# Nine raw chunks in the ring instead of six, four split halves instead of six, and shared slots for two small tiles

## The chip, the cores and the metric

The kernel runs on one core of a Trainium2 chip. The core has TensorE (PE in the profile) with its weight loads (PEld), VectorE (DVE), ScalarE (ACT), GpSimd (POOL) and SyncE (SP), which here mostly issues DMAs. The metric is the device time of one execution in microseconds (us), median of several runs. All weights and activations are fp32.

## The reference

A model of two parts works on one sequence of 512 tokens, 1024 wide. The first part has two layers with a linear recurrence, latent attention and a dense feed-forward; the second has a matrix LSTM mixer and then a mixture of 32 experts, of which each token takes four. The change touches the expert part alone:

```
logits = xt @ w_router + b_router
top_vals, top_idx = top_k(logits, 4);  top_gates = softmax(top_vals)
# per expert e, for the tokens xb routed to it:
gate = min(xb @ w_gate[e] + b_gate[e], 7)
up   = clip(xb @ w_up[e] + b_up[e], -7, 7)
y    = (gate * sigmoid(1.702 * gate) * (up + 1)) @ w_down[e] + b_down[e]
out[token] += top_gate * y
```

Each expert has 12 MB of weights (gate, up and down, each 1024 x 1024 in fp32), so 32 of them are read once each.

## The kernel before

**Experts and blocks.** A router stage counts the tokens of each expert and ranks the experts by count. Each rank has a fixed number of slots: two blocks of 128 slots for the two fullest, then 128 and 64 slots for three, one block of 128 for seven (the last rank, 31, runs first), and one block of 64 for the other twenty. The lists for this case are `FEW` (L1920); a second list stands behind a branch on a flag `many` (L1798, L1801) for inputs with another spread, and is not run here. The order of the ranks is fixed by hand: mostly two 64-slot experts, a 128-slot expert, two 64-slot experts, and then one with two blocks, and so on.

**Chunks and halves.** The weights of an expert are 12 chunks of 1 MB, each a tile of 128 x 2048: four for the first half of gate and up, four for the second, four for down. `split_ahead` (L1583) loads a chunk into the next slot of a ring of `NRAW` tiles named `raw` (DMA on SP's queue, L1591; slots `RAW0` of which lie in a pool opened early) and treats it as two halves.

- For an expert with 128 or more slots each half is *split*: ACT rounds it to a tile `w` in the fast fp32 form of PE (L244) and DVE writes the remainder beside it (L245). These pairs live in a ring of `AHEAD + 1` slots, `EARLY` of which lie in the pool opened early. The products are then whi, wlo and the remainder of x (`product`, `lin`: matmuls at L236, named gu<-w,xth, gu<-w,xtl and dn<-w,hTh, dn<-w,hTl).
- A 64-slot expert (`twin`) multiplies the raw half directly in plain fp32 (gu<-raw,xf and dn<-raw,hf, 128 x 64 columns against 128 x 512), so that it needs no split.

`weights` (L1601) is called once for each half that PE takes. It first tops up the halves in hand to `AHEAD + 1`, counting raw ones too, then emits one or more of the small steps waiting in `later` (`catch_up`), and hands out the oldest half.

**Stages.** `ranked` (L1815) goes through the experts in this order: first half of gate and up of the current expert, down of the one before, second half of gate and up of the current one. Between the matmuls of a stage it places the small steps: `find` (L1513: which tokens, and the gather of their rows from DRAM by POOL, L1529, into xg), `fetch` (L1534: transposes of xg at L1538 into tps, then xf for a 64-slot block, xn for the 64-slot half block of a 128 + 64 expert, xth and xtl for 128 slots) and `turn` (L1690: transposes of the activated product u at L1698 into hf, hn or hTh and hTl). The results `g` (L1668 for a 64-slot expert, L1687 otherwise) and u belong to the activation; yy (L1741, L1760) is the scaled output that POOL scatters into DRAM.

**What sets the order.** PE's instructions stand in the order of the Python code. ACT, DVE, POOL and SP are ordered by a scheduler which simulates the program, and then run in that order, each instruction waiting for its own inputs. A DMA into a ring slot waits on SP until the last reader of that slot is done: PE's last matmul for a raw chunk, DVE's second split for a split chunk. DMAs behind it on SP wait with it.

Of the kernel before, what the change touches and what calls it, by code (L numbers as in the profile page):

```python
# [6 lines left out]
F32 = mybir.dt.float32  # L7
F32R = mybir.dt.float32r
# [9 lines left out]
P = 128  # L18
T = 512
D = 1024  # L20
KD = D // P
# [184 lines left out]
class _Kernel:  # L206
# [1327 lines left out]
    def fetch(self, b):  # L1534


        nc, mo, n = self.nc, self.mo, b["n"]
        turned = lambda tp, k, i: nc.tensor.transpose(tp[:, i * n:(i + 1) * n], b["x"][0:n, k * P:(k + 1) * P],  # L1538
                                                      self.ident[0:n, 0:n])

        def small():
            tp = self.tps()
            for k in range(KD):
                turned(tp, k, k)
            if b["twin"]:
                b["xt"] = xt = mo.tile([P, KD, n], F32, tag="xf", name="xf", bufs=2)
                nc.scalar.activation(xt.rearrange("p k s -> p (k s)"), tp, AF.Copy)  # L1547
            else:
                b["xt"] = xt = mo.tile([P, KD, P], F32R, tag="xn", name="xn", bufs=2)
                self.split(tp.rearrange("p (k s) -> p k s", k=KD), xt[:, :, 0:n], xt[:, :, n:P])  # L1550

        def part(c):
            if c == 0:
                self.nx += 1
                b["xt"] = [x[:, self.nx % 2] for x in self.xts]
            tp = self.tps()
            for k in range(4):
                turned(tp, 4 * c + k, k)
            self.split(tp, *(x[:, 512 * c:512 * c + 512] for x in b["xt"]))

        return [small] if n == 64 else [lambda: part(0), lambda: part(1)]

    def rings(self, z):


        nraw, nw = (NRAW - RAW0, AHEAD + 1 - EARLY) if z else (RAW0, EARLY)
        self.raws += list(self.wp[z].tile([P, nraw, 2048], F32, name="raw").rearrange("p n c -> n p c"))
# [15 lines left out]
    def split_ahead(self, n):  # L1583

        nc = self.nc
        while self.todo and len(self.halves) < n:
            src, i, whole = self.todo.pop(0)
            if i == 0:
                self.raw = self.raws[self.nload % NRAW]
                self.nload += 1  # L1590
                nc.sync.dma_start(self.raw, src)  # L1591
            raw = self.raw[:, 1024 * i:1024 * i + 1024]
            if whole:
                self.halves.append((raw, None))
                continue
            w = self.ws[self.nsplit % (AHEAD + 1)]
            self.nsplit += 1
# [3 lines left out]
    def weights(self):  # L1601
        self.split_ahead(AHEAD + 1)
        self.catch_up(CU + len(self.later) // CV)
        return self.halves.pop(0)
# [85 lines left out]
    def turn(self, blocks, n):  # L1690

        nc, mo = self.nc, self.mo
        self.catch_up()
        for b in blocks:
            m, u = b["n"], b["u%d" % n]
            tp = self.tps()
            for k in range(4):
                nc.tensor.transpose(tp[:, k * m:(k + 1) * m], u[:, k * P:(k + 1) * P], self.ident[0:m, 0:m])  # L1698
            if b["twin"]:
                h = mo.tile([P, 4, m], F32, tag="hf", name="hf", bufs=3)  # L1700
                nc.scalar.activation(h.rearrange("p k s -> p (k s)"), tp[:, 0:256], AF.Copy)
            elif m == 64:
                h = mo.tile([P, 4, P], F32R, tag="hn", name="hn", bufs=2)
                self.split(tp[:, 0:256].rearrange("p (k s) -> p k s", k=4), h[:, :, 0:m], h[:, :, m:P])
            else:
                h = self.pair(mo, [P, T], "hT", bufs=4)
                self.split(tp, *h)
            b["h%d" % n] = h
# [61 lines left out]
    def first_weights(self):  # L1770
# [4 lines left out]
        self.queue(self.chosen[0][0] + self.chosen[0][1])  # L1775
        self.split_ahead(EARLY)

    def experts(self):
# [7 lines left out]
        self.find(b, lambda j: self.gate0[:, j])  # L1786
        self.split_ahead(AHEAD + 1)
        self.down_bias_rows()
# [86 lines left out]
            self.catch_up()  # L1875

    def finish_start(self):
        self.nf = self.mo.tile([P, D], F32, tag="xn", name="nf", bufs=2)
        self.nc.scalar.dma_start(self.nf, self.a["nfrow"].to_broadcast([P, D]))  # L1879

    def finish(self):
# [20 lines left out]

SILU7 = 11.914 / (1.0 + _np.exp(-11.914))
ASIDE = (3, 1)
NRAW = 6
RAW0 = 4
XG = 2
EARLY = 3
CU = 1
CV = 6  # L1910
SGB = 2

AHEAD = 5

SLOTS = [(128, 128)] * 2 + [(128, 64)] * 5 + [(128,)] * 9 + [(64,)] * 15 + [(128,)]

# [55 lines left out]
```

## Time and profile before

| | |
|---|---|
| median of 3 runs | 2970.43 us (2966.03 to 2973.55) |
| profiled execution | 2969.97 us, span on the core 2968.2 us |
| expert part | 1685 to 2941 us of the span |
| PE busy | 2761.0 us, 93% of the span |
| DVE, ACT busy | 1581.2 us (53%), 1119.6 us (38%) |
| raw<-in_wgu, raw<-in_wd | 256 and 128 transfers of 1024 KB; 9.4 and 9.7 us from issue to landing (median) |

Busy PE means that a matmul is in flight, at whichever clock was granted; PE at 93% therefore includes slow matmuls. The expert part is not uniform: the shares of DMA and PE change with the kind of expert, which the table by stretches below shows. In the rows, a number in front is the start in us, the next one how long it lasted, and brackets behind a row give the idle time before it and what released it.

### The profile page before, as it was taken

How to read it: one execution, taken by the hardware profiler on the slowest of the kernel's cores; microseconds unless marked ns; L12 is line 12 of the kernel's file. 1: busy time of each engine (PE TensorE's matmuls, PEld its weight loads, DVE VectorE, ACT ScalarE, POOL GpSimd, SP SyncE). 2: the span in 40 equal slices, each digit the busy share in tenths (PEclk: the TensorE clock that was granted, in tenths of full speed). 3: DMA queues.
4: the chain of work that ended last, by engine and by line, in shares of the span. 5: the costliest groups of instructions: out<-in, count | busy, mean ns of one | idle time of the engine just before them, and what ended most of it. 6: DMA issues, size and time to landing. Idle time of an engine off the chain costs nothing. (4 is left out here: it accounts for less than half of the span.)

```text
span 2968.2 us, 33708 instructions
## 1 busy us (share of the span) xinstructions
PE 2761.0 (93%) x12644; PEld 1936.7 (65%) x12644; DVE 1581.2 (53%) x2601; ACT 1119.6 (38%) x1655; POOL 206.8 (7%) x206
## 2 busy tenths in 40 slices
PE   7999999999999999999999699899899899889885
PEld 5677888888777788888777456454546445446452
DVE  7977575465776653334688543353533434434343
ACT  4644432223564442223353433342423334334342
POOL 0101000000100000000011010111001011010000
PEclk9999999999999999999999799999999999999998
DMA  5332456464221323332214486988987997997997
GB/s 226 122 119 93 156 180 205 142 211 135 86 68 56 95 89 92 100 100 89 89 50 178 172 301 243 405 316 328 382 329 289 398 384 270 404 384 269 394 347 261
DMA packets 126367, 634.93 MB, mean 214 GB/s; under 512 B 14448, under 2 KB 17904, under 8 KB 77040
## 3 DMA queue, kind: packets, MB, share of 16 engines
q1 hardware_dynamic: 111744, 593.94, 53.5%
q0 software_dynamic: 8288, 28.84, 4.3%
q10 hardware_dynamic: 6160, 9.89, 0.9%
q8 instruction: 101, 1.65, 0.2%
q14 instruction: 74, 0.61, 0.1%
HBM read 607.31 MB, written 24.90 MB: 213 GB/s over the span
## 5 line engine op out<-in xcount | busy, mean ns | idle before, releaser
L236 PE MATMUL acc<-hh,whi 128*128 128x512 f32 (+1 forms) x1496 | 576.3, 389 | 15.7 <-ACT hh L506 6.4
L236 PE MATMUL acc<-hh,wlo 128*128 128x512 f32 (+1 forms) x1496 | 578.0, 388 | 5.3 <-DVE wlo L245 5.1
L236 PE MATMUL acc<-hl,whi 128*128 128x512 f32 (+1 forms) x1496 | 575.5, 386 | 0.6 <-DVE hl L507 0.6
L245 DVE TENSOR_TENSOR wlo<-raw,whi 128x1024 fp32r<-128x1024 f32 (+2 forms) x253 | 307.1, 1216 | 268.4 <-ACT whi L244 266.7
L244 ACT ACTIVATE whi<-raw 128x1024 fp32r<-128x1024 f32 (+2 forms) x253 | 258.8, 1024 | 468.9 <-PE acc L236 414.3
L245 DVE TENSOR_TENSOR w<-raw,w 128x1024 fp32r<-128x1024 f32 x288 | 338.6, 1219 | 129.8 <-ACT w L244 128.6
L236 PE MATMUL gu<-w,xth 128*128 128x512 f32 x896 | 319.0, 435 | 45.1 <-ACT w L244 30.8
L236 PEld LDWEIGHTS acc<-hh,whi 128*128 128x128 f32 x1496 | 283.0, 190 | 80.2 <-ACT hh L506 9.1
L236 PEld LDWEIGHTS acc<-hh,wlo 128*128 128x128 f32 x1496 | 284.4, 190 | 62.4 <-DVE wlo L245 6.3
L236 PEld LDWEIGHTS acc<-hl,whi 128*128 128x128 f32 x1496 | 284.5, 190 | 57.3 <-issue 3.1
L236 PE MATMUL gu<-raw,xf 128*64 128x512 f32 x1280 | 312.2, 602 | 1.1 <-ACT xf L1547 0.7
L244 ACT ACTIVATE w<-raw 128x1024 fp32r<-128x1024 f32 x288 | 287.4, 1049 | 51.9 <-DMA raw<-in_wd 18.8
L236 PEld LDWEIGHTS gu<-w,xth 128*128 128x128 f32 x896 | 175.8, 201 | 101.9 <-ACT w L244 44.5
L236 PE MATMUL dn<-raw,hf 128*64 128x512 f32 x640 | 166.2, 631 | 26.5 <-DMA raw<-in_wd 26.3
L236 PE MATMUL gu<-w,xtl 128*128 128x512 f32 x448 | 185.0, 413 | 0.0
L236 PEld LDWEIGHTS gu<-raw,xf 128*64 128x64 f32 x1280 | 83.3, 136 | 129.4 <-issue 118.5
L236 PE MATMUL dn<-w,hTh 128*128 128x512 f32 x448 | 149.2, 410 | 18.3 <-ACT w L244 9.8
L236 PEld LDWEIGHTS dn<-raw,hf 128*64 128x64 f32 x640 | 48.9, 144 | 136.5 <-issue 92.9
L236 PEld LDWEIGHTS dn<-w,hTh 128*128 128x128 f32 x448 | 86.1, 194 | 54.4 <-ACT w L244 15.9
L1669 DVE TENSOR_SCALAR u<-gu 64x512 f32<-64x512 f32 x40 | 27.3, 682 | 168.4 <-ACT g L1668 168.4
L245 DVE TENSOR_TENSOR xtl<-tps,xth 128x512 fp32r<-128x512 f32 x28 | 19.5, 695 | 175.3 <-ACT xth L244 175.3
L828 DVE TENSOR_TENSOR t<-t,acc 128x512 f32<-128x512 f32 x44 | 30.3, 688 | 143.6 <-PE acc L236 134.6
(684 smaller groups left out, 3946.2 us busy)
## 6 DMA issues: line engine op xcount, KB each, us to landing
raw<-in_wgu SPq DMA_DIRECT2D x256, 1024.0 KB, 9.4
raw<-in_wd SPq DMA_DIRECT2D x128, 1024.0 KB, 9.7
raw<-in_ws SPq DMA_DIRECT2D x220, 512.0 KB, 3.5
adaw<-in_wada SPq DMA_DIRECT2D x72, 512.0 KB, 4.9
raw<-in_wada SPq DMA_DIRECT2D x24, 512.0 KB, 3.3
raw<-in_ws SPq DMA_DIRECT2D x24, 384.0 KB, 3.1
xy<-in_xT SPq DMA_DIRECT2D x16, 256.0 KB, 4.8
raw<-in_ws SPq DMA_DIRECT2D x9, 256.0 KB, 2.6
```

The source lines that it names most:

```text
L236: self.nc.tensor.matmul(ps, l, r, start=first, stop=last)
L244: self.nc.scalar.activation(hi, src, AF.Copy)
L245: self.nc.vector.tensor_sub(lo, src, hi.bitcast(F32))
L828: nc.vector.tensor_mul(u, s, ps[1])
L1669: lambda: nc.vector.tensor_scalar(u, p[0:64], 8.0, -6.0, op0=OP.min, op1=OP.max),
```

## The change

Six constants and three tiles change; no formula does.

- `NRAW`: the ring of raw chunks has nine slots, not six; five of them (not four) lie in the early pool.
- `AHEAD`: the halves in hand are four, not six, and with them the ring of split pairs; two of them (not three) lie in the early pool. A pair takes as much memory as a raw chunk.
- `xn` has one buffer instead of two, and the row of the last norm (`nf`), which shares it, too.
- `hn`, of the 64-slot half block, takes slots of `hTh` (four buffers) instead of two of its own.

```diff
                 nc.scalar.activation(xt.rearrange("p k s -> p (k s)"), tp, AF.Copy)
             else:
-                b["xt"] = xt = mo.tile([P, KD, P], F32R, tag="xn", name="xn", bufs=2)
+                b["xt"] = xt = mo.tile([P, KD, P], F32R, tag="xn", name="xn", bufs=1)
...
             elif m == 64:
-                h = mo.tile([P, 4, P], F32R, tag="hn", name="hn", bufs=2)
+                h = mo.tile([P, T], F32R, tag="hTh", name="hn", bufs=4).rearrange("p (k s) -> p k s", k=4)
...
     def finish_start(self):
-        self.nf = self.mo.tile([P, D], F32, tag="xn", name="nf", bufs=2)
+        self.nf = self.mo.tile([P, D], F32, tag="xn", name="nf", bufs=1)
...
-NRAW = 6
-RAW0 = 4
+NRAW = 9
+RAW0 = 5
 XG = 2
-EARLY = 3
+EARLY = 2
...
-AHEAD = 5
+AHEAD = 3
```

Three places show how the order on the engines moves. The first is SP's queue just ahead of the branch on `many`: raw<-in_wgu are chunks of the first expert, raw<-in_ws blocks of a dense weight. Before:

```order
L1591 DMA raw<-in_wgu 128x2048 x4
L256 DMA raw<-in_ws 128x1024
L1591 DMA raw<-in_wgu 128x2048
L256 DMA raw<-in_ws 128x1024
L1591 DMA raw<-in_wgu 128x2048 x2
L1798 TENSOR_LOAD many
L1798 ISA x2
L1801 COMPARE_AND_BRANCH
```

After, at the same place:

```order
L1591 DMA raw<-in_wgu 128x2048 x4
L256 DMA raw<-in_ws 128x1024 x2
L1591 DMA raw<-in_wgu 128x2048 x2
L1798 TENSOR_LOAD many
L1798 ISA x2
L1801 COMPARE_AND_BRANCH
L1827 TENSOR_LOAD order
```

One chunk fewer stands ahead of the branch; it follows behind it.

The second is ACT around the first down stage, that of the 128-slot expert of rank 31, behind the first half of gate and up of a 64-slot expert. The splits (w<-raw) are halves of down; yy at the end is the first output of the stage. Before:

```order
L1547 ACTIVATE xf<-tps 128x512
L1522 ACTIVATE ips<-tps 128x6 x2
L244 ACTIVATE hTh<-tps 128x512
L244 ACTIVATE w<-raw 128x1024 x2
L1668 ACTIVATE g<-gu 64x512
L244 ACTIVATE w<-raw 128x1024 x4
L1760 ACTIVATE yy<-dn,gsl 128x512
```

After:

```order
L1547 ACTIVATE xf<-tps 128x512
L1522 ACTIVATE ips<-tps 128x6 x2
L244 ACTIVATE hTh<-tps 128x512
L1668 ACTIVATE g<-gu 64x512
L244 ACTIVATE w<-raw 128x1024 x6
L1760 ACTIVATE yy<-dn,gsl 128x512
```

The first two splits of the stage stood ahead of g of the 64-slot expert and now stand behind it.

The third is ACT at the start of gate and up of the 128-slot expert in the run of 64-slot experts behind the first expert of 128 + 128 slots (the one behind the second such expert reads alike). The splits are halves of its gate and up, g is that of the 64-slot expert ahead of it. Before:

```order
L1701 ACTIVATE hf<-tps 128x256
L244 ACTIVATE xth<-tps 128x512 x2
L1668 ACTIVATE g<-gu 64x512
L244 ACTIVATE w<-raw 128x1024 x4
L1522 ACTIVATE ips<-tps 128x6
L244 ACTIVATE w<-raw 128x1024 x2
```

After:

```order
L1701 ACTIVATE hf<-tps 128x256
L244 ACTIVATE xth<-tps 128x512
L244 ACTIVATE w<-raw 128x1024
L244 ACTIVATE xth<-tps 128x512
L244 ACTIVATE w<-raw 128x1024
L1668 ACTIVATE g<-gu 64x512
L244 ACTIVATE w<-raw 128x1024 x2
L1522 ACTIVATE ips<-tps 128x6
L244 ACTIVATE w<-raw 128x1024 x2
```

Two splits now stand ahead of g, and only two, not four, between g and ips. At the other starts of this kind g stays ahead of all splits, as in the fence of before.

## Rows read from the trace of the kernel before

**Rows 1.** Busy time by stretch: stretch, length, busy us per engine, granted clock, DMA share.

```profile
core 0: us, PE busy (x) PEld busy (x) DVE busy (x) ACT busy (x) POOL busy (x), PEclk, DMA share, GB/s
...
1846.00:1964.00 118.00, 105.46 (x480) 52.95 (x479) 45.63 (x60) 41.19 (x58) 14.37 (x13) 0.96 0.96 365
1964.00:2046.00 82.00, 79.20 (x350) 49.73 (x350) 41.85 (x53) 34.29 (x47) 6.13 (x4) 0.98 0.78 298
2046.00:2191.00 145.00, 129.35 (x588) 59.69 (x586) 50.79 (x70) 45.97 (x68) 16.96 (x16) 0.96 0.98 380
...
2742.00:2941.00 199.00, 177.55 (x769) 92.71 (x767) 79.81 (x92) 71.32 (x95) 16.86 (x14) 0.93 0.91 349
```

**Rows 2.** Timeline of PE, 64-slot down stages: start us, us, what, idle before.

```profile
2102.33 7.09 PE L236 MATMUL dn<-raw,hf 128*64 128x512 f32 x32
...
1865.96 1.07 PE L236 MATMUL dn<-raw,hf 128*64 128x512 f32 x2 [0.27 <-DMA raw<-in_wd]
...
1877.83 0.64 PE L236 MATMUL gu<-raw,xf 128*64 128x512 f32 x1
...
1878.25 0.59 PE L236 MATMUL dn<-raw,hf 128*64 128x512 f32 x1
...
1878.31 0.96 PE L236 MATMUL gu<-raw,xf 128*64 128x512 f32 x2
...
2758.86 1.02 PE L236 MATMUL dn<-raw,hf 128*64 128x512 f32 x2
...
2770.22 0.96 PE L236 MATMUL gu<-raw,xf 128*64 128x512 f32 x2
```

**Rows 3.** DMA queue 2046 to 2191 us (packets, MB, share); issues 2033 to 2050 us.

```profile
q1 hardware_dynamic: 6972, 50.83, 86.1%
...
L1591 SPq DMA_DIRECT2D raw<-in_wgu x2: 332/332/333, 2033.8 to 2049.0; - x2
```

**Rows 4.** Waits of SP's queue, 1685 to 2941 us: total us, times, longest.

```profile
SPq L1591 <- PE gu L236: 408.0, 155, 16.5
```

**Rows 5.** Waits of PE, 1685 to 2941 us: total us, times, longest.

```profile
PE gu L236 <- ACT w L244: 30.8, 17, 2.2
PE dn L236 <- DMA raw<-in_wd: 26.3, 17, 3.4
PE gu L236 <- DVE w L245: 14.3, 17, 1.1
```

**Rows 6.** Timeline of ACT and PE: a usual start; the first down stage.

```profile
2084.30 0.59 ACT L1668 ACTIVATE g<-gu 64x512 f32<-64x512 f32 x1 [1.33 <-PE gu L236]
...
2085.14 2.00 ACT L244 ACTIVATE w<-raw 128x1024 fp32r<-128x1024 f32 x2 [0.24 <-DMA raw<-in_wgu]
...
2086.24 0.80 PE L236 MATMUL gu<-w,xth 128*128 128x512 f32 x1 [2.04 <-ACT w L244]
...
1731.31 2.00 ACT L244 ACTIVATE w<-raw 128x1024 fp32r<-128x1024 f32 x2
```

**Rows 7.** Timeline of ACT, DVE and PE, down stage of a 128-slot expert.

```profile
2135.78 5.78 ACT L244 ACTIVATE w<-raw 128x1024 fp32r<-128x1024 f32 x6
...
2137.24 6.88 DVE L245 TENSOR_TENSOR w<-raw,w 128x1024 fp32r<-128x1024 f32 x6
...
2139.76 0.62 PE L236 MATMUL dn<-w,hTh 128*128 128x512 f32 x2
...
2141.12 0.63 PE L236 MATMUL dn<-w,hTh 128*128 128x512 f32 x2
```

**Rows 8.** Gathers (L1529), 1685 to 2941 us; timeline of one and its use.

```profile
L1529 POOL DMA_INDIRECT xg<-H,idx x36: 936/1007/1815, 1713.2 to 2867.6; - x36
...
DMA to landing us min/median/max: 5.3/8.5/11.4
...
2755.48 1.00 POOL L1529 DMA_INDIRECT xg<-H,idx  x1 [2.89 <-DVE idx L1527]
...
2775.74 0.66 PE L1538 MATMUL tps<-cst,xg 128*128 128x128 f32 x4
```

## The prediction

> **What bounds the kernel now.** I began with busy time by stretch [rows 1]. The change touches only the expert part, 1685 to 2941 us. Two kinds of stretch alternate there. Where a wide expert runs (two blocks of slots; 1964 to 2046 is one of five such), PE is busy 79.2 of 82 us, and the DMA engines idle a good fifth of the time (share 0.78). Where 64-slot experts stand in pairs around a 128-slot one, which I call a run (there are five, 1846 to 1964 first and 2742 to 2941 last, three rows shown), the DMA share is 0.91 to 0.99 and PE loses 13 to 21 us in each. The reason is in the code: a 64-slot expert multiplies raw weights, 32 matmuls for 4 chunks in 7.09 us [rows 2], so it eats a chunk of 1 MB in 1.8 us. In 2046 to 2191 the raw queue moved 50.83 MB [rows 3]: 50.83 / 1.0486 = 48.5 chunks in 145 us, 2.99 us each. So the ring of six drains in such a run, and it is full, with SP waiting for a free slot, before it: SP's waits for gate_up matmuls alone are 408 us [rows 4], and around 2040 us two issues in a row stand at 2033.8 and 2049.0 us [rows 3], a hole of 15.2 us in which landings ran out. That bandwidth is lost for lack of a slot.
>
> PE's own waits [rows 5] come in two families: down products for wd chunks in flight (26.3 us, 17 times), and starts of a split stage for the first whi and wlo (30.8 + 14.3 us at gate_up). The second is hardly a matter of data: ACT first does g of the 64-slot expert, which needs that expert's last matmul, then (0.24 us of it for the chunk) the split at 2085.14, and PE starts at 2086.24 [rows 6].
>
> **Three more chunks in the ring.** A 64-slot down stage that does not wait takes 7.09 us. Eight stages do wait. The first runs from 1865.96 to 1878.31, less one stray gate matmul between (1877.83 to 1878.25), so 11.9, 4.8 over; the last from 2758.86 to 2770.22, so 10.9, 3.9 over [rows 2]. By the same reading the eight lose, run by run, 4.8; 4.4 + 5.2; 4.2 + 6.1; 4.0 + 6.8; 3.9: 39.4 us, idle time plus the matmuls at the lower clock level behind it (granted clock 0.93 to 0.96 in these runs [rows 1]). With nine slots the transfers go on through the hole before each run: three chunks more lie ready when it starts. At 2.99 us each that is 9.0 us by which everything behind lands earlier, as the queue never stops after that. A run cannot gain more than it loses: min(9.0, loss) = 4.8 + 9.0 + 9.0 + 9.0 + 3.9 = 35.7 us. The wide stretches can pay for the refill: a share of 0.78 over 82 us leaves 18 us of engine time [rows 1], and three chunks need 9. Bounds: 0 if nothing is banked; 39.4 if the 128-slot expert in the middle refills the ring too. I take 35.7, by the row that measures a chunk in the run itself.
>
> The Trainium skill, page "DMA: Bandwidth & Descriptors", section Specifications, gives about 358 GB/s for one core's HBM and 435 for the fabric. The row has 380 GB/s over 145 us [rows 1], above the first, so it is no ceiling here; an estimate by 358 is 2.93 us a chunk and 35.1 us in all instead of 35.7.
>
> **Four halves as parts, not six.** ACT may now start a split only when PE has left the half four places back, not six. The tightest place is a 128-slot down stage: six splits run on ACT without a break from 2135.78, 0.96 us each, the fifth at 2139.6, the sixth at 2140.5 [rows 7]. PE goes from the first half to the second at 2139.76 and is through the second at 2141.12, 1.36 us a half [rows 7], so the fifth split would start 0.2 to 0.4 us and the sixth 0.6 to 0.8 us later. DVE hides that: it works through the six wlo from 2137.24 at 1.15 us each and reaches the fifth at 2141.8 and the sixth at 2143.0, when ACT would be done at 2141 and 2142.3. I take 0. In gate_up of a 128-slot expert the order on ACT already holds the fifth split back behind ips, and in wide stages a half serves two blocks, an estimated 1.36 us for the 128 slots and most of that again for the second block, longer than ACT plus DVE (0.96 + 1.15). Without that cover each of the 21 stages of 128-slot experts would lose some 0.8 us, 17 us: the bound from above. Below nothing it cannot go.
>
> **What moves.** Ahead of the branch SP issues six chunks instead of seven, and the seventh comes just behind it, while PE has six chunks to work through first: 0. The third split of the first weights moves from the router stage to the rank stage, where ACT waits for PE: 0. In the first down stage two splits stood before g (1731.31 [rows 6]) and now stand behind it: PE gets the 2.0 us start wait that all others have, and some slow matmuls: +2.5. At two gate_up starts (the 128-slot expert behind each of the two widest) two splits now stand ahead of g: -2.5 where the chunk has landed, which I grant the first (its run has 9.0 - 4.8 us in hand) and not the second. Sum 0. Single buffers for xn and slots of hTh for hn: the experts that use them stand at least two 64-slot experts apart, 0.
>
> **Sum.** The profiled execution took 2969.97 us, 1.8 outside its span of 2968.2, and 0.5 under the median of 2970.43. 2969.97 - 35.7 + 2.5 - 2.5 = 2934.
>
> **Rivals.** *Two chunks, not three* (0.15): with fewer parts a raw chunk of a split expert is freed up to one chunk later against PE, so only two more lie ready: 6.0 us a run, 4.8 + 6.0 x 3 + 3.9 = 26.7, 2943. For: such slots do wait for DVE's split, six halves ahead of PE before and four now. Against: a wide down stage has its last split done well before the next 64-slot stage. *All stalls go* (0.08): 39.4 and both early starts, 5.0 - 2.5, give 2928; for it speaks that transfers slacken a little in the 128-slot part; against, the share of 0.98.
>
> *A deeper queue slows its transfers* (0.12): if eight or nine chunks in flight took 5% longer each, 3.14 for 2.99 us, the five runs' 253 chunks at most (their 756 us by the 2.99 of one run) would take 253 x 0.15 = 38 us more: 2972, no change. For: none of the rows has more than six in flight. Against: the rate holds where six are.
>
> *Gathers wait behind the raw queue: slower* (0.07). A block's gather lands 8.5 us after issue at the median, 11.4 at most; in the tightest case it is issued at 2755.48 and used at 2775.74, 20.3 us later [rows 8]. If a gather had to let a full ring of nine pass, 9 x 2.99 = 27 us, it would be late by 6.7 us there; 16 of the 36 gathers have 20.3 to 24.8 us, so about 4.4 us late in the mean: 16 x 4.4 = 70, less 36: 3004. It decides from a landing time of 20.3 us. Against: with about five chunks ahead of it at 3 us, the gather did not take 15 us.
>
> The Trainium skill, same page, section Queues, rings and completion order, says that each DMA engine takes turns between its queues, a packet at a time. By that rule this rival is void; the median of 8.5 us agrees. I leave it 0.07.
>
> **Chances.** Forecast 0.58 (2934), two chunks 0.15, all stalls 0.08, no change 0.12, slower 0.07. A measurement of this kernel can tell about 0.3%, 9 us, from nothing. Faster by more: 0.58 + 0.15 + 0.08 = 0.81; same 0.12; slower 0.07. The range takes in the three faster cases with their unknowns: from 2920 (the 2928 case and another 8 us, if early chunks also shorten the other start waits) to 2961 (two chunks and the 17 us of the split bound); 0.19 lies in cases above it.
>
> **What will show it.** Right: the eight down stages near 7.1 us and PE's wait for wd under 5 us; the hole at 2040 us filled, shares of 0.85 and more in wide stretches; the expert part near 1220 us; waits for whi still near 30. Wrong: wd waits above 15 us although the hole is gone (then the rate, not the bank, is the limit), new waits of PE for wlo inside 128-slot stages, or PE transposes waiting for xg. What would upset it most is a chunk time above 2.99 us.

## The result and the profile after

| | before | after |
|---|---|---|
| median | 2971.99 us (4 runs, 2966.03 to 2975.56) | 2917.01 us (4 runs, 2914.68 to 2921.05) |
| profiled execution | 2969.97 us, span 2968.2 | 2914.68 us, span 2912.9 |

The ratio is 0.9827, with a 95% interval from 0.9804 to 0.9849: 55 us less, where the prediction said 36. The forecast, 2934, was 17 us too high, and 2917 lies 3 us below the lower end of the range (2920); the direction was as forecast.

The waits of PE in the expert part of the changed kernel (total us, times, longest), to be read beside [rows 5]:

```profile
PE gu L236 <- ACT w L244: 29.4, 17, 1.9
PE gu L236 <- DVE w L245: 14.8, 17, 1.1
PE dn L236 <- ACT w L244: 11.5, 7, 1.6
PE dn L236 <- ACT yb L1413: 11.1, 2, 9.4
PE dn L236 <- DVE w L245: 7.9, 7, 1.1
```

The row of 26.3 us for wd chunks is gone. The starts of split stages wait as before, 29.4 and 14.8 us at gate_up. The groups by line say the same of the matmuls of the 64-slot down stages. First the row of the page of before, then that of after (count, busy us, mean ns, idle before):

```profile
L236 PE MATMUL dn<-raw,hf 128*64 128x512 f32 x640 | 166.2, 631 | 26.5 <-DMA raw<-in_wd 26.3
```

```profile
L236 PE MATMUL dn<-raw,hf 128*64 128x512 f32 x640 | 143.0, 600 | 0.0
```

Idle time of 26.5 us has become 0, and busy time fell by 23.2 us too: a matmul counts as busy for part of the time in which the next weight load waits for its chunk, and part of the work ran at a lower clock (last section). A stage that was broken up by waits, as those of [rows 2], now runs in one piece (timeline of PE, after):

```profile
2054.31 7.04 PE L236 MATMUL dn<-raw,hf 128*64 128x512 f32 x32
```

Busy time by stretch, after, cut at the same places of the program as [rows 1] (same columns):

```profile
1846.00:1956.00 110.00, 101.78 (x477) 52.06 (x475) 45.12 (x60) 41.25 (x58) 19.55 (x13) 0.97 0.97 374
1956.00:2038.00 82.00, 79.59 (x352) 49.88 (x354) 42.83 (x53) 35.27 (x47) 5.70 (x4) 0.98 0.82 321
2038.00:2173.00 135.00, 125.66 (x586) 60.39 (x586) 51.24 (x70) 46.26 (x68) 15.94 (x16) 0.95 1.00 390
...
2696.00:2886.00 190.00, 171.35 (x768) 89.30 (x766) 79.74 (x92) 72.26 (x96) 16.87 (x14) 0.96 0.91 349
```

The runs of 64-slot experts got shorter (118 to 110, 145 to 135, 199 to 190 us), the wide stretch between the first two did not (82 and 82).

To account for the gain I cut the PE timeline into stages, from the first matmul of one stage to the first of the next, and compare the profiled executions:

| stages | before | after | difference |
|---|---|---|---|
| all up to the second gate_up of the first 64-slot expert (starts at) | 1745.7 | 1746.0 | +0.3 |
| 64-slot down (20) | 193.1 | 151.9 | -41.2 |
| 64-slot gate_up (from there on) | 384.9 | 372.7 | -12.2 |
| split stages of gate_up (from there on) | 429.6 | 426.0 | -3.6 |
| split stages of down (from there on) | 187.8 | 189.1 | +1.3 |

The sum is -55.4 us; the spans differ by 55.3.

### The profile page after: what moved, and what is told of

Same layout as the page of the kernel before. It is cut to its first block, busy times and chain, and to the rows that moved or that the text cites. A ratio compares the mean times of both kernels' runs of the same rounds, so it can differ in the third digit from the quotient of the medians.

```text
span 2912.9 us, 33755 instructions
## 1 busy us (share of the span) xinstructions
PE 2732.2 (94%) x12644; PEld 1927.9 (66%) x12644; DVE 1584.0 (54%) x2601; ACT 1124.3 (39%) x1655; POOL 212.3 (7%) x206
## 5 line engine op out<-in xcount | busy, mean ns | idle before, releaser
L236 PE MATMUL acc<-hh,whi 128*128 128x512 f32 (+1 forms) x1496 | 574.4, 388 | 13.6 <-ACT hh L506 6.2
L236 PE MATMUL gu<-w,xth 128*128 128x512 f32 x896 | 314.9, 431 | 44.2 <-ACT w L244 29.4
L244 ACT ACTIVATE w<-raw 128x1024 fp32r<-128x1024 f32 x288 | 293.6, 1052 | 117.3 <-PE gu L236 70.4
L236 PEld LDWEIGHTS acc<-hh,wlo 128*128 128x128 f32 x1496 | 283.2, 189 | 62.2 <-DVE wlo L245 6.3
L236 PE MATMUL gu<-raw,xf 128*64 128x512 f32 x1280 | 306.2, 602 | 1.2 <-ACT xf L1547 0.7
L236 PE MATMUL dn<-raw,hf 128*64 128x512 f32 x640 | 143.0, 600 | 0.0
L1669 DVE TENSOR_SCALAR u<-gu 64x512 f32<-64x512 f32 x40 | 27.3, 682 | 159.6 <-ACT g L1668 159.6
L236 PEld LDWEIGHTS gu<-w,xtl 128*128 128x128 f32 x448 | 88.7, 198 | 20.3 <-DVE many L1392 0.2
## 6 DMA issues: line engine op xcount, KB each, us to landing
raw<-in_wgu SPq DMA_DIRECT2D x256, 1024.0 KB, 12.5
```

What stands on the lines that cost most here:

```text
L236: self.nc.tensor.matmul(ps, l, r, start=first, stop=last)
L244: self.nc.scalar.activation(hi, src, AF.Copy)
L1669: lambda: nc.vector.tensor_scalar(u, p[0:64], 8.0, -6.0, op0=OP.min, op1=OP.max),
```

## The experiments

Each kernel is the changed one with the edit shown. Times are medians; the ratio is to the kernel before in runs of the same session. Between kernels of different sessions the ratios compare better than the medians, as the kernel before itself took 2965 to 2972 us in them. "Loss" is the time of the eight 64-slot down stages that used to wait, over 8 x 6.87 us, the length each has in the changed kernel, read from the timeline of PE as in the table above.

| kernel | slots / halves | median us | ratio, 95% interval | loss us |
|---|---|---|---|---|
| before (profile) | 6 / 6 | 2971.99 | 1 | 40.7 |
| e11, shared tiles alone | 6 / 6 | 2967.39 | 0.9997 (0.9983 to 1.0011) | about 40 |
| e1 | 6 / 4 | 2971.54 | 1.0004 (0.999 to 1.0019) | 47.5 |
| e2 | 7 / 4 | 2942.40 | 0.9912 (0.9885 to 0.9938) | 27.3 |
| e4 | 7 / 6 | 2940.75 | 0.9917 (0.9891 to 0.9943) | 20.6 |
| e3 | 8 / 4 | 2927.49 | 0.9862 (0.9835 to 0.9888) | 10.5 |
| **the change** | 9 / 4 | 2917.01 | 0.9827 (0.9804 to 0.9849) | 0 |
| e12 | 9 / 3 | 2910.55 | 0.9796 (0.9774 to 0.9818) | 7.4 |
| e5 | 10 / 3 | 2900.24 | 0.9774 (0.9744 to 0.9805) | 0 |
| e9, order edge | 6 / 6 | 2936.88 | 0.9902 (0.9872 to 0.9932) | 43.2 |
| e6, order edge | 9 / 4 | 2891.21 | 0.9747 (0.9717 to 0.9777) | 17.4 |
| e8, order edge | 10 / 3 | 2866.96 | 0.9667 (0.9635 to 0.9698) | 15.7 |
| e10, order edge | 11 / 2 | 2907.19 | 0.9791 (0.9773 to 0.9809) | 0 |

**Is it the ring?** The ring goes back to six slots, all else stays:

```diff
-NRAW = 9
-RAW0 = 5
+NRAW = 6
+RAW0 = 4
```

> The changed kernel with the ring of raw chunks put back to six (four in the early pool); four split halves and the shared small tiles stay. Theory (the ring alone carries the gain): the eight 64-slot down stages wait for chunks in flight again, PE's wait for wd is back near 26 us, and the time near 2970 us, that of the kernel before (2972), give or take 6. Rival (the shorter split ring or the moved splits gave part of it): 2960 us or less. Second rival (four halves cost something that the ring hid): 2980 us or more.

The time is that of the kernel before, and PE's wait is back:

```profile
PE dn L236 <- DMA raw<-in_wd: 27.1, 19, 3.4
```

So the other edits together are worth nothing without the slots (the interval is 0.999 to 1.0019): the ring carries the gain. The shared tiles alone (e11) were tried too, with both rings as before:

> The kernel before with the shared small tiles alone (xn with one buffer, hn in slots of hTh), six raw chunks and six split halves. All theories: the time of the kernel before within 6 us, since the experts that use these tiles stand far apart. If it is faster by 10 us or more, my account of the whole gain by the ring is too large by that.

0.9997: nothing that these runs can tell, as expected.

**What is a slot worth?** Two kernels between six and nine.

```diff
-NRAW = 9
+NRAW = 7
```

> The changed kernel with seven raw chunks. Theory by stage (each stalled stage gets a chunk's time for itself, because the ring refills in the 128-slot expert between the two 64-slot pairs): with nine slots the last two chunks of the eight stages landed 3.6 to 6.1 us before their use; two chunks less take 5.9 us off (2.93 us each), so waits of 0 to 2.3 us come back, 7.8 in all, and some slow matmuls: about 2930 us (2925 to 2935). Theory by run, that of the prediction (one bank for each run, 15 us a slot over five runs): 2917 + 30 = 2947 us.

The same with `NRAW = 8`:

> The changed kernel with eight raw chunks. By stage: one chunk less takes 2.9 us off leads of 3.6 us and more, so nearly nothing waits: 2917 to 2921 us. By run: 2917 + 15 = 2932 us.

2942 and 2927 lie between the two theories, both nearer to "by run" (2947 and 2932). The stages themselves speak for "by stage" in part: the loss falls by 20.2 us from six to seven slots and by 16.8 from seven to eight. A bank for each of the five runs could take off 5 x 2.80 = 14.0 at most per slot, a chunk's time for each of the eight stages 22.4 (2.80 us a chunk is worked out below); the loss also holds the slow matmuls behind a wait, so this is no sharp test. What "by stage" had wrong is the lead. I counted a chunk as there with its last packet; the landing that the profile gives came 1.4 us later (median), so the leads were shorter by that. With eight slots one down stage still waits (loss 5.8 us of the 10.5), and the 64-slot gate_up stages take 381.4 us as with six and seven, and 372.7 only with nine. PE's waits with eight name the chunks of gate_up too:

```profile
PE gu L236 <- DMA raw<-in_wgu: 3.9, 7, 1.5
PE dn L236 <- DMA raw<-in_wd: 3.7, 2, 3.5
```

Neither theory is right as a formula. From six to seven slots the two stages of the third run lost 6.7 us less together and those of the fourth 6.3, more than one chunk's time, and the one of the first run 0.4; that the 128-slot expert in the middle refills part of the ring is how I read it.

**What do four halves cost?** Seven slots with six halves, beside e2:

```diff
-NRAW = 9
-RAW0 = 5
+NRAW = 7
+RAW0 = 4
 XG = 2
-EARLY = 2
+EARLY = 3
...
-AHEAD = 3
+AHEAD = 5
```

> Seven raw chunks and six split halves as before the change (three in the early pool, four raw chunks there); the small tiles shared. It stands beside the run with seven chunks and four halves. Theory (four halves cost nothing, since DVE's split hides ACT's later start): the same within 5 us. Rival (the 0.8 us a stage that I gave as the bound): faster by up to 17 us. Second rival (a longer split ring frees raw chunks earlier, so that a slot is worth more): waits of the 64-slot down stages shorter than with four halves, and 3 to 8 us faster.

The time is the same (0.9917 and 0.9912) within intervals of some 8 us either way, as the first theory had it; the 17 us of the rival are excluded, 3 us are not. But the stages show an effect as in the prediction's rival "two chunks, not three": with four halves the loss is larger by 6.7 us at seven slots (27.3 and 20.6) and by 6.8 at six (47.5 and 40.7). The reason that the rival gives fits: a raw chunk is freed later when its split comes later. PE's wait for wd chunks with seven slots, first four halves, then six:

```profile
PE dn L236 <- DMA raw<-in_wd: 16.6, 10, 2.8
```

```profile
PE dn L236 <- DMA raw<-in_wd: 11.8, 9, 2.1
```

In the profiled executions part of the 6.7 us comes back elsewhere (the 64-slot gate_up stages take 2.8 less with four halves, and the second stage of the first 64-slot expert starts 2.5 earlier), and 3.2 remain (2943.88 and 2940.64); I did not follow this further.

**One step further.** Ten slots, three halves, at the same memory:

```diff
-NRAW = 9
+NRAW = 10
...
-AHEAD = 3
+AHEAD = 2
```

> The changed kernel with the trade carried one step further at the same memory: ten raw chunks, three split halves. The steps so far were 6 to 7: 29 us, 7 to 8: 15, 8 to 9: about 10, and with nine no 64-slot down stage waits for a chunk. Theory (the ring's gain ends where the waits end): the tenth slot brings 0 to 3 us. Theory on the halves (DVE's split, 1.15 us, and ACT's, 0.96, still cover a half of 1.36 us on PE): three cost 0 to 3 us. So 2912 to 2922 us. Rival (three halves are too few: the fourth split waits for PE, up to 0.8 us in each of 21 stages): 2925 to 2935 us, with PE's waits for wlo above 40 us at the split stages.

A miss in my favour: 2900, 12 us under the expected span. As no down stage of the changed kernel waits, I suspected the order that comes with three halves, and ran three halves with nine slots (`AHEAD = 2` alone):

> Nine raw chunks as in the changed kernel, but three split halves instead of four: ten chunks and three halves took 2900 us, 17 less than the changed kernel, though no 64-slot down stage of the changed kernel waits for a chunk. Theory (the order that comes with three halves gave it: the rows of the down bias on PE no longer wait 9.4 us for ACT's yb ahead of the branch, and at the two starts behind the experts of 128 + 128 slots the splits go on): 2900 to 2905 us. Rival (the tenth slot gave it): 2915 to 2920 us.

2910, between the two; its interval overlaps with both neighbours, so the traces have to tell. With three halves PE's rows of the down bias stand elsewhere ahead of the branch. In the changed kernel their wait is this (PE and ACT), and behind it the same rows with ten slots and three halves (e5):

```profile
1704.64 1.28 PE L236 MATMUL dn<-bdr,gT 96*128 96x512 f32 x2 [9.36 <-ACT yb L1413]
...
1703.99 1.08 ACT L1413 ACTIVATE yb<-dn 128x512 f32<-128x512 f32 x2 [9.56 <-DMA accd<-yb]
```

```profile
1697.08 0.50 PE L236 MATMUL dn<-bdr,gT 96*128 96x512 f32 x1 [1.72 <-ACT yb L1413]
```

ACT's yb waited 9.56 us for its buffer, which a write to DRAM still held. In the stage table e12 and e5 are 4.0 and 4.2 us ahead of the changed kernel at 1746: that is the order's part. e12 then loses 7.4 us in one down stage for want of a chunk, and e5 none: that is the tenth slot's. The largest part I can put to neither: the split stages take 10.2 us less in e12 than in the changed kernel and 9.7 less in e5. Part of it is the clock: the down stage of the changed kernel that starts at 2348.7 has a granted clock of 0.88 and takes 14.5 us, the same stage of e12 has 1.00 and takes 13.0. Why PE kept the higher level there with three halves stays open.

**Are the start waits a matter of data?** PE's 63.6 us at the starts of split stages are the largest waits left. The edit lets ACT issue g of a 64-slot expert behind the second split of the stage that follows, an order edge (a fixed order of two instructions on one engine) and nothing else; `self.splits`, kept by lines that are not shown, lists ACT's splits in their order:

```diff
-        self.later += [lambda: nc.scalar.activation(g, p[64:P], AF.Silu, scale=1.702),
+        def silu():
+            if self.halves and self.halves[0][1] is not None:
+                with self.tc.issue_after(self.splits[-len(self.halves) + 1]):
+                    nc.scalar.activation(g, p[64:P], AF.Silu, scale=1.702)
+            else:
+                nc.scalar.activation(g, p[64:P], AF.Silu, scale=1.702)
+
+        self.later += [silu,
```

> The changed kernel, with ACT's first two splits of every split stage put ahead of g of the 64-slot expert in ACT's order (an order edge alone). In the changed kernel PE waits 29.4 + 11.5 us for the first whi and 14.8 + 7.9 us for the first wlo of 24 stages, 63.6 us, and the chunk landed 3.3 us or more before PE's start. Theory (the wait is the order on ACT): some 1.8 us less at each of about 19 starts, 34 us, so about 2883 us; PE's waits for whi under 10 us. Rival (inside a run of 64-slot experts the transfers set the pace, share 0.99 to 1.00, leads of 1 to 4 us over the landing): what PE gains there comes back as waits for chunks, and only the starts in and next to wide stretches pay: 10 to 15 us, 2902 to 2907 us.

2891, 26 us less than the changed kernel (24 by the ratios); between theory and rival. The waits show both at work:

```profile
PE gu L236 <- ACT w L244: 20.8, 15, 2.1
PE gu L236 <- DVE w L245: 12.7, 17, 0.8
...
PE dn L236 <- DMA raw<-in_wd: 9.9, 8, 3.3
```

The starts wait less, and a wait for chunks that was gone is back: loss 17.4 us, all of it in the second stalled stage of the middle three runs (4.4, 6.2, 6.8). The run that stands at 2038 to 2173 us in the changed kernel shortened by 1.5 us only. The transfers set its pace: its DMA share and its rate are those of the changed kernel, 1.00 and 390 GB/s, though the granted clock rose from 0.95 to 0.99:

```profile
2030.00:2164.00 134.00, 124.80 (x587) 58.00 (x583) 50.73 (x70) 46.14 (x67) 15.94 (x16) 0.99 1.00 390
```

Elsewhere the edge paid twice: PE waited less, and the granted clock was higher (0.98 over the expert part instead of 0.96, last section).

The same edge with ten slots and three halves, and with the rings of before:

> The same order edge with ten raw chunks and three split halves. If the rival of the run before holds (transfers set the pace in the runs), the tenth slot gives back up to 3 us at each of the eight stages: 10 to 20 us faster than the same edge with nine. If the order alone sets it, as fast as that run within 4 us.

> The kernel before in its rings (six raw chunks, six split halves) with the same order edge and the shared small tiles. Theory (without the larger ring the chunks land too late, so that ACT waits for the chunk instead of g and the down stages wait longer by what the starts gain): within 8 us of the kernel before. Rival (the start wait is independent of the ring): faster by the same 30 us or so as with nine slots.

With ten slots 24 us less than with nine, more than the 10 to 20 of the rival, but not for its reason: the loss fell by 1.7 us only. In the profiled executions, 31 us apart (that of ten slots is the fastest of its four), 13.6 us stand ahead of the second stage of the first 64-slot expert, which starts at 1731.2 instead of 1744.8, and the granted clock of the expert part rose once more, to 0.99. With the rings of before it is 0.9902, 28 us: my theory that the chunks would come too late is refuted. The loss stays (43.2 and 40.7), but PE's start waits fall from 62.2 us to 40.8, and the granted clock of the expert part rises from 0.95 to 0.98. That the chunks do not come later may be because PE, done earlier with a chunk, frees its slot earlier; no run tests this. Edge and ring nearly add up. 2867 us, 0.9667 of the kernel before, is the best of these kernels.

**How few halves?** Eleven slots, two halves, with the edge (`NRAW = 11`, `RAW0 = 6`, `EARLY = 1`, `AHEAD = 1`):

> Eleven raw chunks, two split halves, with the order edge (splits ahead of g); the neighbour is ten and three with the same edge, 2867 us. Theory (where the split ring binds): with two halves a split starts when PE has left the half two places back, and ACT plus DVE take 0.96 + 1.15 = 2.1 us against 1.36 us of PE for the half in between, some 0.75 us lost at six of eight halves of 21 stages: 95 us, about 2960 us, with PE's waits for wlo above 60 us inside the stages of 128-slot experts, and none in the wide stages. Rival (the eleventh slot is worth as much as the tenth and the splits stay covered): 2850 to 2870 us.

2907, 40 us slower than ten and three (37 by the ratios); no down stage waits for a chunk, and the split ring binds:

```profile
PE gu L236 <- DVE w L245: 30.5, 57, 0.8
PE gu L236 <- ACT w L244: 21.2, 12, 5.1
PE dn L236 <- DVE w L245: 16.0, 21, 0.8
```

With three halves and the edge PE waited for wlo 16 times at gate_up (11.9 us), now 57 times; 46.5 us in all where I had expected over 60, and less than half the loss of 95. The cover that the prediction named (DVE's split) is used up between three and two halves.

## Why the prediction was right in kind and small in size

**The hidden cost of fewer halves, 0: right as far as these runs can tell.** e4 and e2 agree in time within some 8 us, and PE's waits for wlo at gate_up did not grow: 14.3 us with six halves, 14.8 with four, 14.2 and 15.9 with three (e5, e12). This agrees with DVE hiding it, down to three halves.

**What moves, sum 0: right as a sum, with parts I had not seen.** The first down stage with its neighbour took 3.9 us more (8.41 + 12.31 before, 10.12 + 14.51 after) where I said 2.5. The first 64-slot stage started 3.6 us earlier (1725.0 and 1721.4), which the text did not have; the two cancel, so the 0 was in part luck. Of the early starts I granted 2.5 us to the first and nothing to the second; the two stages around each gave 1.6 and 2.3. But the same two stages of the three runs without an early start gave 1.7, 0.8 and 3.7, so this says little; PE's start waits themselves (whi and wlo) fell by 0.9 us at the first and by 0.2 at the second.

**The bank of three chunks, 35.7 us: the step that failed, a term that was too small.** The 64-slot down stages and the gate_up stages next to them gave 41.2 + 12.2 = 53.4 us, 17.7 more. The first two of the following made it too small, and the third belongs to the second.

1. *The loss was read too narrowly.* I counted a stage from its first matmul to the end of its last. A gate_up stage ahead ends with the wait for the first wd chunk, and one of the stages behind waits for gate_up chunks of the same late queue. Two rows of before that I had not looked at (PE; PEld, which waits first):

```profile
2301.10 1.07 PE L236 MATMUL dn<-raw,hf 128*64 128x512 f32 x2 [1.79 <-DMA raw<-in_wd]
...
2079.08 0.20 PEld L236 LDWEIGHTS gu<-raw,xf 128*64 128x64 f32 x4 [1.32 <-DMA raw<-in_wgu]
```

The three stages ahead that changed gave 3.3 us, the eight behind 6.9, three others 1.9: the 12.2. In the other seven behind, waits for chunks are small or absent. What they have in common is a slow start: the first four matmuls and the two of the bias come one at a time, and the transposes behind them start 2.0 us after the first matmul instead of 1.2. One of them, before and then after:

```profile
2178.51 0.64 PE L236 MATMUL gu<-raw,xf 128*64 128x512 f32 x1
...
2180.53 0.46 PE L1698 MATMUL tps<-cst,u 64*128 64x64 f32 x4
```

```profile
2161.15 1.03 PE L236 MATMUL gu<-raw,xf 128*64 128x512 f32 x4
...
2162.32 0.46 PE L1698 MATMUL tps<-cst,u 64*128 64x64 f32 x4
```

Seven times 0.85 us is most of the 6.9. The slow start is gone in the changed kernel, where the down stages ahead no longer stall; how the two hang together stays open.

2. *The cap of 9.0 us for a run.* The runs with two stalled stages had lost 9.6, 10.3 and 10.8 us by my reading and got all of it back. So a run got more than a bank of three chunks; the 128-slot expert in between, as I read it, refills the ring in part.

3. *2.99 us a chunk was not the pace of the transfers.* The stretch from 2046 us takes in the end of the hole. Behind it the queue of the raw chunks did this (packets, MB, share), before (2053 to 2191 us), after (2045 to 2173) and with the order edge (2037 to 2164):

```profile
q1 hardware_dynamic: 6937, 50.55, 89.9%
```

```profile
q1 hardware_dynamic: 6576, 47.89, 90.4%
```

```profile
q1 hardware_dynamic: 6516, 47.45, 90.6%
```

50.55 MB in 138 us are 2.86 us a chunk, 47.89 in 128 are 2.80, 47.45 in 127 are 2.81. Put into the same sum, 2.80 gives less, 33.9 us instead of 35.7. What the single figure hid is that the time per chunk falls with more slots: over the 46 chunks of the stretch these rows make 46 x 0.06 = 2.8 us, an estimate, and with the bank of 8.4 that is 11.2 us for a run, above the 9.6 to 10.8 that could be lost.

**The signs.** PE's wait for wd under 5 us: right, none is left. Waits for whi near 30: right. Expert part near 1220 us: 1678.0 to 2885.7 is 1207.7. A hole filled: wrong, and it was the wrong sign to give. Two issues of wd chunks in the changed kernel still stand 10.0 us apart, 2030.6 and 2040.6, since the ring is full; it is just full with nine:

```profile
2030.64 10.31 SPq L1591 DMA_DIRECT2D raw<-in_wd  x2
```

Shares of 0.85 in wide stretches: right in two of five. They are 0.77, 0.82, 0.79, 0.89 and 0.92, where before had 0.77, 0.78, 0.72, 0.79 and 0.77.

**The rivals.** *All stalls go* (2928) came nearest and had the right mechanism, with the loss too small. *Two chunks, not three*: 7 us on the stalls, and on the time nothing that these runs can tell. *A deeper queue slows its transfers*: landing took longer, 12.5 us instead of 9.4 at the median for wgu chunks, but because more are queued; the time per chunk fell from 2.86 to 2.80 us. *Gathers wait*: their landing took 9.1 us at the median and 13.3 at most, against 20.3 us that the tightest of before had:

```profile
DMA to landing us min/median/max: 4.5/9.1/13.3
```

The Trainium skill, page "DMA: Bandwidth & Descriptors", section "Queues, rings and completion order", says that each engine takes turns between queues by the packet; the trace agrees, with gathers that land in 9.1 us beside a queue of up to nine chunks, which take 25 us at 2.80 each.

## What to carry to other kernels

When a stage waits for a stream, add up what the whole neighbourhood loses, weight loads and the stages on either side included, and not the waits of the stage alone. A ring's next slots were worth 29, 15 and 10 us here (the seventh, eighth and ninth), less each time, and no simple count of runs or stages gave these numbers. A slot can be paid for with buffers whose producer has time in hand; the point where that cover ends (here between three and two halves) has to be measured. A wait that looks like data can be order: one edge on ACT was worth about as much at six slots as at nine. And when a pace is read from a stretch, the stretch has to hold the same part of the program in both kernels, and no hole at its edge.

## What was not expected of the hardware

Behind the hole the core moved 394 GB/s over 138 us with six slots and 403 over 128 us with nine; the 380 of [rows 1], a stretch that takes in the end of the hole, was no ceiling. Neither the order edge nor a tenth slot raised the 403 by more than 1 in the same run (403 and 404). Before and after:

```profile
2053.00:2191.00 138.00, 122.35 (x550) 57.08 (x546) 50.10 (x69) 43.16 (x63) 15.07 (x14) 0.96 1.00 394
```

```profile
2045.00:2173.00 128.00, 118.66 (x548) 57.75 (x544) 50.56 (x69) 43.86 (x63) 14.05 (x14) 0.95 1.02 403
```

The Trainium skill, page "HBM Reference", section "Specifications (TRN2)", says that a core that streams alone reaches about 425 GB/s, above its share of 358; the 403 is above that share too, and no stretch of a whole run here comes to 425.

A wait cost more than the idle time that PE's rows show. In the kernel before, PE is idle for 26.5 us in the 64-slot down stages, but the weight loads ahead of the matmuls waited 43.3 us for the same chunks:

```profile
L236 PEld LDWEIGHTS dn<-raw,hf 128*64 128x64 f32 x640 | 48.9, 144 | 136.5 <-issue 92.9 <-DMA raw<-in_wd 43.3
```

In five of the eight stages the granted clock fell as well, to between 0.84 and 0.88 of full speed over the stage (1.2 GHz, the lower level, for part of it), and in three it did not. The longest idle time of PE in the five was 1.5 to 3.4 us, in the three 1.3 to 1.95. Two of them (busy time by stretch, before; columns as in [rows 1]):

```profile
2062.70:2074.20 11.50, 8.99 (x35) 2.45 (x33) 1.36 (x2) 0.59 (x1) 0.00 (x0) 1.00 1.01 422
...
2633.30:2647.00 13.70, 9.89 (x32) 2.61 (x30) 1.37 (x2) 0.59 (x1) 0.00 (x0) 0.88 1.02 391
```

The clock is also a part of the gain, one that the waits do not show. The expert part behind 1746 us in the kernel before, in the changed one and with the order edge (from 1745 us):

```profile
1746.00:2941.00 1195.00, 1100.20 (x4890) 602.17 (x4886) 484.91 (x614) 421.18 (x577) 111.48 (x97) 0.95 0.89 341
```

```profile
1746.00:2885.00 1139.00, 1073.08 (x4889) 596.59 (x4890) 488.17 (x614) 426.21 (x577) 117.76 (x97) 0.96 0.91 354
```

```profile
1745.00:2861.00 1116.00, 1063.62 (x4889) 585.61 (x4888) 486.54 (x614) 424.99 (x577) 119.73 (x97) 0.98 0.93 363
```

What is missing to full speed, 0.05 x 1195, 0.04 x 1139 and 0.02 x 1116, is some 60, 46 and 22 us. This is an estimate from above, since PE stood idle for part of the time at the lower level: up to 14 of the 55 us of the change were clock, and up to 24 behind the order edge.
